# A two-layer mixer trunk in fp32 by split halves: the sample's output projection in seven half products, with the scale by token and the first results moved between engines

## The chip, the cores and the metric

The kernel runs on one core of one Trainium2 chip. The metric is the device time of one execution, in microseconds. The engines are TensorE (PE, with PEld for its weight loads), VectorE (DVE), ScalarE (ACT), GpSimd (POOL) and SyncE (SP), which issues most DMAs.

## The reference

A prompt of 512 tokens and a sample of 1024 tokens go through the same two layers, in fp32, width 1024:

```python
hn = rmsnorm(h, ln1[i])
z = hn @ w_in[i]
q, k, v, ga, uf, gf, mga, mgf = jnp.split(z, SPLIT_IDX, axis=-1)
...
a = band_attention(q, k, v, sink[i]) * jax.nn.silu(ga)
f = fourier_mix(uf, w_fmix[i]) * jax.nn.silu(gf)
merged = jax.nn.sigmoid(mga) * (a @ w_ao[i]) + jax.nn.sigmoid(mgf) * (f @ w_fo[i])
h = h + merged @ w_out[i]
gate = jax.nn.sigmoid(rmsnorm(h, ln_pg[i]) @ w_pg[i])
h = h + (p[i].astype(h.dtype) @ w_pe[i]) * gate
```

After the layers a last RMSNorm gives the outputs. The attention is banded (128 tokens to each side), the Fourier branch is a two-dimensional transform by channel groups.

## The kernel before, in words

Activations lie with features on the 128 partitions and tokens along the row: a tile is 128x512, eight of them (KD) make the 1024 features of a chunk of 512 tokens. Chunk 0 is the prompt, chunks 1 and 2 (PAIR) the sample. Each fp32 operand is split in two parts (`hi_lo`): ACT casts the high half (L93), DVE or POOL subtracts it to give the low half (L94). A product of a 128x128 weight tile and a token tile is then three matmuls, high by high, high by low, low by high (L105, L106, L107 in `mm3_steps`).

A layer runs the prompt and then the sample. Stages of the sample: the input projection (L236), attention and Fourier mixing woven into it, then `merge` (L553 on). The input projection already uses seven half products in place of eight: class `Pair` takes two output tiles by two chunks as a 2x2 block product, with weight sums S1 to S4 and token sums T1 to T4, and adds the products' banks on DVE (L253, L257 and others).

`merge` first makes the branch products, for each output tile m and chunk c 12 matmuls for attention (`ao`) and 12 for Fourier (`fo`). DVE applies the gates (L568, L569) and adds the two (L576) into `merged`. Then the 16 merged tiles are split. The output projection follows: for each m and chunk 24 matmuls in one PSUM bank, 384 a layer, and DVE adds a quarter of the bank to the old h (L594), the residual. `Norm.add` squares each new tile on ACT (L325) and sums the squares on DVE or POOL (L327, L330). The new h is split for the gate (L311 ACT, L312 DVE), and the gate's product runs as another 384 matmuls for both chunks; `finish` (L605 to L614) scales it by token (L610), applies tanh and adds the per-layer input (L612, L614). The scale by token is a row of 1/rms spread over the partitions by transposes into a PSUM bank (`Norm.scale_ps`) and copied to SBUF by DVE (L368). In the last layer `result` scales h for the output: for m%3 == 2 ACT multiplies by the norm's weight and POOL by the scale (L628, L629), else one DVE instruction (L631).

Weights of all these stages come from one stream (class `Weights`): DMAs of 4x128 rows by SP, split a few tiles ahead, `w_out` of the sample by POOL. The Tile framework sets the order of instructions of each engine from a timeline of its own at build time; `keep_in_program_order` pins some. PSUM has banks mm (3), sc (2), o (1) and misc (2); `any_ps` takes mm, sc and o in turn. `tick()` and `run` interleave other work, such as the prompt's normalizing for the next layer (L373), as steps.

## Time and profile before

| | us |
|---|---|
| median of 3 runs | 2195.79 (2192.51, 2195.79, 2196.96) |
| the profiled execution | 2191.9, of which its span 2190.1 |
| PE busy in the span | 2165.7 in 10273 matmuls |
| DVE, ACT, POOL busy | 1482.8, 1092.0, 284.6 |

The profile is of one execution, which took 2191.9 us, 3.9 less than the median; 1.8 us of it lie outside the span. The mean clock granted to PE is 0.999 of full speed. By the times of L594 the sample's output projection runs from about 952 to 1037 in layer 0 and from about 2001 to 2085 in layer 1. Busy times count matmuls by their modelled ends; how close together they start is read from the timeline.

### The profile page before, as it was taken

The page shows a single profiled execution, that of the slowest core. Times are in us where ns is not written, and L with a number is a line of the kernel's source. Part 1 is how long each engine was busy: PE and PEld are TensorE (multiplying, and loading weights), DVE is VectorE, ACT ScalarE, POOL GpSimd, SP SyncE. Part 2 cuts the span into 40 slices and gives each one's busy share as a digit, 9 for nine tenths or more (in the row PEclk, how much of TensorE's full clock was granted, in tenths as well). Part 3 has the DMA queues.
Part 4 walks back from the last instruction along what each step waited for, and adds up shares of the span by engine and source line. Part 5 has one row for each costly group of instructions (what it writes and reads, how often), then busy time and mean ns, then how long its engine had stood idle before and what let it go on. Part 6 is the DMA issues. An engine that isn't in the chain of part 4 may idle for free. (4 is left out here: it accounts for less than half of the span.)

```text
span 2190.1 us, 30146 instructions
## 1 busy us (share of the span) xinstructions
PE 2165.7 (99%) x10273; PEld 1806.4 (82%) x10273; DVE 1482.8 (68%) x2836; ACT 1092.0 (50%) x2338; POOL 284.6 (13%) x212
## 2 busy tenths in 40 slices
PE   9999999999999999999999999999999999999998
PEld 7878787888888888888888888888888888888887
DVE  5866686676678883464556676867766787855385
ACT  6576433566665464134324864336666644612252
POOL 0201100000002112221400010000000011241232
PEclk9999999999999999999999999999999999999999
DMA  8746454544448576531446455543444574753152
GB/s 313 265 136 205 171 192 145 166 140 137 159 142 290 198 251 213 199 105 64 151 159 202 152 193 172 185 153 130 161 146 151 192 283 137 267 197 116 44 169 100
DMA packets 242187, 380.71 MB, mean 174 GB/s; under 512 B 21233, under 2 KB 97649, under 8 KB 242033
## 3 DMA queue, kind: packets, MB, share of 16 engines
q1 hardware_dynamic: 234704, 365.80, 49.7%
q10 hardware_dynamic: 7328, 12.98, 1.6%
q8 instruction: 81, 1.33, 0.2%
q14 instruction: 74, 0.60, 0.1%
HBM read 270.17 MB, written 108.53 MB: 173 GB/s over the span
## 5 line engine op out<-in xcount | busy, mean ns | idle before, releaser
L236 PE MATMUL mm<-act,act 128*128 128x512 f32 x2856 | 692.6, 392 | 2.5 <-DVE scr L253 1.8
L236 PEld LDWEIGHTS mm<-act,act 128*128 128x128 f32 x2856 | 530.8, 188 | 111.2 <-ACT act L93 2.7
L105 PE MATMUL mm<-act,act 128*128 128x512 f32 x1384 | 542.9, 392 | 3.7 <-ACT scr L485 2.8
L107 PE MATMUL mm<-act,act 128*128 128x512 f32 x1384 | 541.2, 391 | 1.8 <-DVE act L94 1.8
L106 PE MATMUL mm<-act,act 128*128 128x512 f32 x1384 | 541.1, 391 | 0.0
L93 ACT CAST act<-act 128x512 fp32r<-128x512 f32 x574 | 329.1, 619 | 182.0 <-DMA act<-in_w_af 69.6
L94 DVE TENSOR_TENSOR act<-act,act 128x512 fp32r<-128x512 f32 x474 | 321.6, 713 | 33.8 <-ACT act L93 32.0
L107 PEld LDWEIGHTS mm<-act,act 128*128 128x128 f32 x1384 | 260.3, 188 | 56.9 <-DVE act L94 4.4
L105 PEld LDWEIGHTS mm<-act,act 128*128 128x128 f32 x1384 | 260.6, 188 | 56.4 <-ACT scr L485 4.2
L106 PEld LDWEIGHTS mm<-act,act 128*128 128x128 f32 x1384 | 260.5, 188 | 50.8
L93 ACT CAST act<-scr 128x512 fp32r<-128x512 f32 (+1 forms) x260 | 152.8, 615 | 127.7 <-DVE scr L435 58.0
L94 DVE TENSOR_TENSOR act<-scr,act 128x512 fp32r<-128x512 f32 x256 | 174.9, 704 | 51.6 <-ACT act L93 50.1
L94 POOL TENSOR_TENSOR act<-act,act 128x512 fp32r<-128x512 f32 x100 | 140.5, 1430 | 311.6 <-ACT act L93 249.3
L923 POOL TENSOR_TENSOR scr<-scr,scr 128x512 f32<-128x512 f32 x24 | 34.4, 1435 | 1036.6 <-DVE scr L920 1012.9
L325 ACT ACTIVATE scr<-act 128x512 f32<-128x512 f32 x103 | 63.8, 632 | 211.2 <-DVE act L594 142.6
L94 DVE TENSOR_TENSOR act<-misc,act 128x512 fp32r<-128x512 f32 x132 | 88.1, 685 | 72.0 <-ACT act L93 71.6
L93 ACT CAST act<-misc 128x512 fp32r<-128x512 f32 x132 | 73.9, 587 | 121.4 <-PE misc L909 119.2
L885 ACT ACTIVATE act<-act,stat 128x385 f32<-128x385 f32 (+1 forms) x192 | 110.6, 579 | 29.7 <-DVE stat L882 29.1
L882 DVE CUSTOM_DVE_ANT_0 act<-sc,mask_sb,nsink_sb 128x384 f32<-128x384 f32 (+1 forms) x192 | 104.2, 568 | 29.8 <-PE sc L874 29.2
L105 PE MATMUL sc<-act,act 128*128 128x512 f32 (+1 forms) x316 | 118.9, 376 | 0.0
L106 PE MATMUL sc<-act,act 128*128 128x512 f32 (+1 forms) x316 | 118.0, 374 | 0.0
L107 PE MATMUL sc<-act,act 128*128 128x512 f32 (+1 forms) x316 | 118.0, 373 | 0.0
(228 smaller groups left out, 2627.1 us busy)
## 6 DMA issues: line engine op xcount, KB each, us to landing
act<-in_w_in SPq DMA_DIRECT2D x136, 256.0 KB, 4.3
act<-in_w_in SPq DMA_DIRECT2D x68, 512.0 KB, 4.5
gt<-scr SPq DMA_DIRECT2D x96, 256.0 KB, 2.7
scr<-gt SPq DMA_DIRECT2D x96, 256.0 KB, 5.0
act<-in_w_pg SPq DMA_DIRECT2D x80, 256.0 KB, 3.4
act<-in_w_af SPq DMA_DIRECT2D x64, 256.0 KB, 5.3
act<-in_w_out SPq DMA_DIRECT2D x64, 256.0 KB, 5.1
pl<-scr ACTq DMA_DIRECT2D x48, 256.0 KB, 3.0
```

The source lines that it names most:

```text
L93: S.copy(hi, src)
L94: lo_eng.tensor_tensor(lo, src, f(hi), op=ALU.subtract)
L105: keep(PE.matmul(out, wh, xh, start=i == 0, stop=False))
L106: PE.matmul(out, wh, xl, start=False, stop=False)
L107: PE.matmul(out, wl, xh, start=False, stop=i == n - 1)
L236: PE.matmul(bank, w, v, start=first and k == 0 and n == 0, stop=k == 3 and n == 2, skip_group_check=True)
L325: S.activation(sq, h, AF.Square)
L882: V.tensor_tensor_reduce(out=pr[:, :W], in0=sc[:, :W], in1=msk, scale=-0.125, scalar=nsink_sb[:, l, head : head + 1], op0=ALU.add, op1=ALU ...
L885: S.activation(pr, pr, AF.Exp, bias=nmx[:, e], scale=-1.0, accum_out=rs[:, e])
L923: G.tensor_tensor(a2, a2, gate, op=ALU.mult)
```

## The change

For the sample, `merge` makes all attention halves first (L664 writes the gated product), then all Fourier halves (L666, L667). As the merged tiles of two chunks arrive, `made(m)` builds the token sums (L627 T1, L634 T2, L639 T3, L642 T4; rows 0 to 3 are tiles m and m+4) and splits them (L95 ACT, L96 DVE). The output projection is four calls of `Pair.alone`, each two output tiles by two chunks in seven half products of 12 matmuls (L237), 336 in a layer; DVE adds the banks (L291, L298, L299, L303, L307), then does the residual (L681). The weight sums and splits (`Pair.prepare`, L217 to L225, L96) are DVE's. The gate's weights come from a second stream whose first two steps fall in the last pair (`GATE_AT`), split by POOL. The scale for the gates is copied by ACT (L410); the first chunks' results read it from its bank, all on DVE (L731). In the input projection the sum c+v is made one product sooner. In the order of PE the 128x512 matmuls go from 8462 to 8366; in DVE's, 181 rows more.

```diff
@@ -222,22 +227,27 @@
...
+        def product(self, p, x, lead, pinned=False):
             def product(i, bank, xs, first):
                 if i == 2:
                     self.load(p + 1)
                 self.prepare(7 * p + i + lead)
                 for k, ((wh, wl), (xh, xl)) in enumerate(zip(self.w[7 * p + i], x[xs])):
                     for n, (w, v) in enumerate(((wh, xh), (wh, xl), (wl, xh))):
...
+            return product
+
...
@@ -252,14 +262,46 @@
...
+            V.tensor_tensor(v, c, v, op=ALU.add)
             yield from product(4, a, "B21", False)
             finish(0, 0, a, False)
-            V.tensor_tensor(v, c, v, op=ALU.add)
             finish(1, 1, v, True)
             yield
             yield from product(5, b, "T4", False)
             V.tensor_tensor(s1, b, s1, op=ALU.add)
             finish(1, 0, s1, True)
...
+        def alone(self, p, x, finish, lead):
+
+            a, b, c, d = (any_ps() for _ in range(4))
+            product = self.product(p, x, lead, True)
+            yield from product(0, a, "B11", True)
+            s1 = scr()
+            S.copy(s1, a)
+            yield
+            yield from product(1, c, "T1", True)
+            yield
+            yield from product(2, b, "T2", True)
+            q = scr()
+            V.tensor_tensor(q, b, s1, op=ALU.add)
+            yield
+            yield from product(3, a, "B21", False)
+            finish(0, 0, a, False)
+            yield
+            yield from product(4, b, "T3", False)
+            v = scr()
+            V.tensor_tensor(v, b, s1, op=ALU.add)
+            V.tensor_tensor(s1, c, v, op=ALU.add)
+            finish(1, 1, s1, True)
+            yield
+            yield from product(5, d, "T4", True)
+            V.tensor_tensor(v, d, v, op=ALU.add)
+            finish(1, 0, v, True)
...
@@ -567,35 +609,96 @@
...
+            pairs, t1 = Pair(outs_w, ("A11", "S1", "S2", "A12", "S3", "A22", "S4")), {}
+            late_rows = []
+            sums = {n: [] for n in ("B11", "T2", "T1", "T3", "B21", "T4", "B22")}
+
+            def made(m):
+                (b11, b12), (b21, b22) = (
+                    [merged[c][k // 2][:, k % 2, :] for c in chunks] for k in (m % 4, m % 4 + 4 if m > 3 else m % 4))
+                if m < 4:
+                    sums["B11"].append(two(halves(b11, V)))
+                    t1[m] = b11
+                    V.tensor_tensor(t1[m], b12, b11, op=ALU.subtract)
+                    sums["T1"].append(two(halves(t1[m], V)))
+                    return
+                late_rows.append((t1[m - 4], b12, b21, b22))
+                if m == 4 or m == 6:
+                    return
+                for t2, _, _, b22 in late_rows:
+                    V.tensor_tensor(t2, b22, t2, op=ALU.subtract)
+                    sums["T2"].append(two(halves(t2, V)))
+                for _, _, b21, _ in late_rows:
+                    sums["B21"].append(two(halves(b21, V)))
+                for _, b12, _, b22 in late_rows:
+                    V.tensor_tensor(b12, b22, b12, op=ALU.subtract)
+                    sums["T3"].append(two(halves(b12, V)))
+                for t2, _, b21, _ in late_rows:
+                    V.tensor_tensor(b21, b21, t2, op=ALU.subtract)
+                    sums["T4"].append(two(halves(b21, V)))
+                for _, _, _, b22 in late_rows:
+                    sums["B22"].append(two(halves(b22, V)))
+                late_rows.clear()
+
+            for i in range(2):
+                for m in range(KD):
                     if m % 2 == 0:
...
+                    n = KD * i + m - AHEAD
+                    if n == 0:
+                        pairs.load(0)
+                    if n > 1:
+                        pairs.prepare(min(n - 2, 4))
+                    for c in chunks:
+                        if i == 0 and m % 2 == 0:
+                            merged[c].append(big([P, 2, T]))
+                        g, s, out = scr(), merged[c][m // 2][:, m % 2, :], bank()
+                        SY.dma_start(g, GT[c][2 * m + i])
+                        mm3(out, w[m % 2 * 4 :][:4], parts[c][4 * i :][:4])
+                        if i == 0:
+                            V.scalar_tensor_tensor(s, g, 1.0, out, op0=ALU.add, op1=ALU.mult)
+                        else:
+                            V.scalar_tensor_tensor(g, g, 1.0, out, op0=ALU.add, op1=ALU.mult)
+                            V.tensor_tensor(s, s, g, op=ALU.add)
+                        tick()
+                        yield
+                    if i:
+                        made(m)
         hs, norm, rb = {c: [] for c in chunks}, {c: Norm() for c in chunks}, {}
...
+
+        def residual(m, c, out, in_sbuf=False):
+            old = scr()
+            SY.dma_start(old, x[c, m] if l == 0 else H[c][m])
+            if m // 2 == len(hs[c]):
+                hs[c].append(big([P, 2, T]))
+            h = hs[c][m // 2][:, m % 2, :]
+
+            V.scalar_tensor_tensor(h, out, 0.25, old, op0=ALU.mult, op1=ALU.add)
+            norm[c].add(h)
+
...
+        else:
+            following = gate_ws.start()
+            for p in range(KD // 2):
+                for n, _ in enumerate(pairs.alone(p, sums, lambda i, j, out, sb: residual(2 * p + i, chunks[j], out, sb), 3)):
+                    if p == KD // 2 - 1 and n in GATE_AT:
+                        next(following, None)
+                    tick()
+                    yield
+            ws = gate_ws
...
@@ -361,11 +403,11 @@
-        def scale(self):
+        def scale(self, copy=V.tensor_copy):
             rb_ps = pst("misc")
             self.scale_ps(rb_ps)
             rb = scr()
-            V.tensor_copy(rb, rb_ps)
+            copy(rb, rb_ps)
             return rb
@@ -604,7 +707,7 @@
-                rb[c] = norm2[c].scale()
+                rb[c] = norm2[c].scale(S.copy)
@@ -618,17 +721,14 @@
...
 
-            r = norm[c].scale()
+            r = pst("misc")
+            norm[c].scale_ps(r)
             for m in range(KD):
                 after(1 + m // 2, lambda m=m: result_tile(c, m, r))
 
         def result_tile(c, m, r):
             o, h, g = scr(), hs[c][m // 2][:, m % 2, :], ln_sb[:, 4, m : m + 1]
-            if m % 3 == 2:
-                S.activation(h, h, AF.Copy, scale=g)
-                G.tensor_tensor(o, h, r, op=ALU.mult)
-            else:
-                V.scalar_tensor_tensor(o, h, g, r, op0=ALU.mult, op1=ALU.mult)
+            V.scalar_tensor_tensor(o, h, g, r, op0=ALU.mult, op1=ALU.mult)
             SY.dma_start(y[c, m], o)
 
         keep = tc.keep_in_program_order
```

Two places of the order of instructions, both in layer 0. First, DVE where the branch products end and the output projection begins. `act_` and `scr_` are SBUF tiles, `mm_`, `sc_`, `o_` PSUM banks. Before, from the last gated products (L569) through the last sum and splits to the first residuals (L594):

```order
L569 SCALAR_TENSOR_TENSOR scr_9094<-scr_9094,mm_9098 128x512
L94 TENSOR_TENSOR act_9153<-act_8593,act_9153 128x512
L94 TENSOR_TENSOR act_9156<-act_8745,act_9156 128x512
L576 TENSOR_TENSOR act_9049<-scr_9093,scr_9094 128x512
L94 TENSOR_TENSOR act_9159<-act_8745,act_9159 128x512
L94 TENSOR_TENSOR act_9162<-act_8897,act_9162 128x512
L94 TENSOR_TENSOR act_9165<-act_8897,act_9165 128x512
L94 TENSOR_TENSOR act_9168<-act_9049,act_9168 128x512
L94 TENSOR_TENSOR act_9171<-act_9049,act_9171 128x512
L594 SCALAR_TENSOR_TENSOR act_9210<-sc_9183,scr_9184 128x512
```

Every split stands ahead of the first residual, and nothing else comes between. In the change, from the last T4 sum to the sum c+v of the first pair (L299); `act_9264` is the low half of A22 of the first pair, `o_9232` its bank c:

```order
L642 TENSOR_TENSOR act_8759<-act_8759,act_8602 128x512
L96 TENSOR_TENSOR act_9213<-act_8619,act_9213 128x512
L96 TENSOR_TENSOR act_9217<-act_8759,act_9217 128x512
L681 SCALAR_TENSOR_TENSOR act_9299<-sc_9230,scr_9297 128x512
L96 TENSOR_TENSOR act_9221<-act_8759,act_9221 128x512
L96 TENSOR_TENSOR act_9224<-act_8776,act_9224 128x512
L96 TENSOR_TENSOR act_9227<-act_8776,act_9227 128x512
L96 TENSOR_TENSOR act_9264<-act_8678,act_9264 128x512
L298 TENSOR_TENSOR scr_9318<-mm_9231,scr_9246 128x512
L96 TENSOR_TENSOR act_9282<-scr_8794,act_9282 128x512
L96 TENSOR_TENSOR act_9303<-act_9260,act_9303 128x512
L299 TENSOR_TENSOR scr_9246<-o_9232,scr_9318 128x512
```

The splits of late token sums now run on beside the first products, with the banks' sums (L298, L299), a residual (L681) and weight splits (`act_9264`, `act_9282`, `act_9303`) between and behind them.

Second, DVE in the middle of the output projection. Before, residuals, splits of the prompt's tiles for the next layer (L94) and sums of squares (L330):

```order
L594 SCALAR_TENSOR_TENSOR act_9410<-mm_9383,scr_9384 128x512
L94 TENSOR_TENSOR act_9416<-act_7286,act_9416 128x512
L94 TENSOR_TENSOR act_9460<-act_7444,act_9460 128x512
L330 TENSOR_TENSOR scr_9258<-scr_9258,scr_9412 128x512
L94 TENSOR_TENSOR act_9519<-act_7444,act_9519 128x512
L594 SCALAR_TENSOR_TENSOR act_9378<-sc_9428,scr_9429 128x512
L330 TENSOR_TENSOR scr_9212<-scr_9212,scr_9456 128x512
L594 SCALAR_TENSOR_TENSOR act_9410<-mm_9463,scr_9464 128x512
```

Here only L594 belongs to the product itself. In the change, the first half of the third pair:

```order
L291 TENSOR_TENSOR scr_9587<-mm_9531,scr_9549 128x512
L681 SCALAR_TENSOR_TENSOR act_9607<-o_9530,scr_9605 128x512
L96 TENSOR_TENSOR act_9612<-act_9568,act_9612 128x512
L372 TENSOR_TENSOR scr_9301<-scr_9301,scr_9609 128x512
L298 TENSOR_TENSOR scr_9627<-mm_9531,scr_9549 128x512
L299 TENSOR_TENSOR scr_9549<-sc_9532,scr_9627 128x512
L681 SCALAR_TENSOR_TENSOR act_9632<-scr_9549,scr_9630 128x512
L303 TENSOR_TENSOR scr_9627<-mm_9533,scr_9627 128x512
L217 TENSOR_TENSOR scr_9637<-act_9569 128x512
L372 TENSOR_TENSOR scr_9325<-scr_9325,scr_9634 128x512
L681 SCALAR_TENSOR_TENSOR act_9607<-scr_9627,scr_9656 128x512
L96 TENSOR_TENSOR act_9640<-scr_9637,act_9640 128x512
```

The residual reads a bank or a sum from SBUF, the prompt's tiles are gone from here, and weight sums (L217) and splits (L96) have come in.

## Rows read from the trace of the kernel before

**Rows 1.** The page, parts 1 and 2: busy time; PE and clock in slices
```profile
PE 2165.7 (99%) x10273; PEld 1806.4 (82%) x10273; DVE 1482.8 (68%) x2836; ACT 1092.0 (50%) x2338; POOL 284.6 (13%) x212
...
PE   9999999999999999999999999999999999999998
...
PEclk9999999999999999999999999999999999999999
```

**Rows 2.** PE's waits: line, awaited, total us, times, longest us
```profile
PE o L914 <- ACT act L93: 4.1, 4, 1.5
PE mm L105 <- ACT scr L485: 2.8, 4, 1.1
PE mm L107 <- DVE act L94: 1.8, 4, 0.6
PE mm L236 <- DVE scr L253: 1.8, 2, 0.9
```

**Rows 3.** Windows in both output projections: us, busy by engine, PEclk, DMA share, GB/s
```profile
960.00:1040.00 80.00, 80.00 (x355) 66.27 (x354) 40.81 (x62) 31.23 (x54) 18.66 (x15) 1.00 0.19 64
2000.00:2080.00 80.00, 80.00 (x354) 66.25 (x353) 27.27 (x39) 21.93 (x38) 21.11 (x16) 1.00 0.23 75
```

**Rows 4.** Groups by line: PE, layer 0, branch products to gate
```profile
L105 PE MATMUL mm<-act,act 128*128 128x512 f32 x273 | 106.6, 391 | 0.0
```

**Rows 5.** Timeline of PE: start, duration; first and last of eight matmuls
```profile
1749.72 0.39 PE L106 MATMUL mm<-act,act 128*128 128x512 f32 x1
...
1751.31 0.39 PE L107 MATMUL mm<-act,act 128*128 128x512 f32 x1
```

**Rows 6.** Timeline of DVE: start, duration, line; instructions that wait for nothing
```profile
1334.74 1.88 DVE L94 TENSOR_TENSOR act<-act,act 128x512 fp32r<-128x512 f32 x3
...
1744.78 3.20 DVE L94 TENSOR_TENSOR act<-act,act 128x512 fp32r<-128x512 f32 x5
1747.89 0.68 DVE L253 TENSOR_TENSOR scr<-mm,scr 128x512 f32<-128x512 f32 x1
```

**Rows 7.** The page, part 5: count, busy us, mean ns, idle before
```profile
L93 ACT CAST act<-act 128x512 fp32r<-128x512 f32 x574 | 329.1, 619 | 182.0 <-DMA act<-in_w_af 69.6
L94 DVE TENSOR_TENSOR act<-act,act 128x512 fp32r<-128x512 f32 x474 | 321.6, 713 | 33.8 <-ACT act L93 32.0
...
L94 POOL TENSOR_TENSOR act<-act,act 128x512 fp32r<-128x512 f32 x100 | 140.5, 1430 | 311.6 <-ACT act L93 249.3
```

**Rows 8.** Groups by line: layer 0's output projection, the scale's copy
```profile
L368 DVE COPY scr<-misc 128x512 f32<-128x512 f32 x1 | 0.7, 678 | 0.0
```

**Rows 9.** Single lines: durations in ns, least/median/longest
```profile
L631 DVE SCALAR_TENSOR_TENSOR scr<-act,ln_sb,scr x12: 742/744/1884, 1930.8 to 2171.7; 128x512 f32<-128x512 f32 x12
...
L629 POOL TENSOR_TENSOR scr<-act,scr x4: 1289/1292/1738, 1930.9 to 2159.3; 128x512 f32<-128x512 f32 x4
...
L612 DVE SCALAR_TENSOR_TENSOR scr<-scr,scr x46: 673/692/1775, 807.3 to 2166.5; 128x512 f32<-128x512 f32 x46
```

**Rows 10.** Window in layer 0's gate, columns as rows 3
```profile
1040.00:1126.00 86.00, 86.00 (x393) 71.41 (x392) 48.30 (x77) 27.19 (x46) 23.08 (x18) 1.00 0.44 150
```

**Rows 11.** Windows at a fall of the clock, columns as rows 3
```profile
201.00:202.00 1.00, 0.64 (x2) 0.54 (x3) 1.00 (x3) 1.00 (x4) 1.00 (x2) 0.50 1.01 377
...
204.00:206.00 2.00, 2.00 (x9) 1.61 (x8) 1.76 (x7) 1.61 (x4) 0.00 (x0) 0.92 0.85 211
```

**Rows 12.** Timeline of PE there; in brackets idle time and releaser
```profile
201.36 0.79 PE L105 MATMUL mm<-act,act 128*128 128x512 f32 x1 [1.06 <-ACT scr L485]
...
202.38 0.63 PE L107 MATMUL mm<-act,act 128*128 128x512 f32 x1
202.81 0.63 PE L105 MATMUL mm<-act,act 128*128 128x512 f32 x1
```

**Rows 13.** Window with POOL busy, layer 1's prompt, columns as rows 3
```profile
1900.00:1910.00 10.00, 10.00 (x46) 8.29 (x45) 9.62 (x8) 4.73 (x10) 9.66 (x6) 1.00 0.64 199
```

**Rows 14.** Groups by line: DVE, layer 0, branch products to gate
```profile
L94 DVE TENSOR_TENSOR act<-act,act 128x512 fp32r<-128x512 f32 x38 | 29.8, 817 | 2.5 <-issue 1.3 <-ACT act L93 1.0
```

More of the change, by code (lines that the diff above doesn't have):

```diff
@@ L29 @@
 LAST = 2
+AHEAD = 4
+GATE_AT = (4, 8)
 NF = 2
@@ L235, in product, with steps @@
                     for n, (w, v) in enumerate(((wh, xh), (wh, xl), (wl, xh))):
-                        PE.matmul(bank, w, v, start=first and k == 0 and n == 0, stop=k == 3 and n == 2,
-                                  skip_group_check=True)
+                        ins = PE.matmul(bank, w, v, start=first and k == 0 and n == 0, stop=k == 3 and n == 2,
+                                        skip_group_check=True)
+                        if pinned and k == n == 0:
+                            tc.keep_in_program_order(ins)
                     if k == 1:
                         yield
+            return product
+        def steps(self, p, x, finish, lead):
+            a, b, c = pst("mm"), pst("mm"), pst("mm")
+            product = self.product(p, x, lead)
             yield from product(0, a, "B11", True)
@@ L262, in steps @@
             finish(1, 0, s1, True)
+            yield
+            yield from product(6, c, "B22", False)
+            V.tensor_tensor(q, c, q, op=ALU.add)
+            finish(0, 1, q, True)
+            yield
[24 more added lines that the diff above has]
+            finish(1, 0, v, True)
             yield
@@ L551, in mixed, with merge @@
             yield
-    def merge(l, chunks, parts, ws, bank, groups):
+    def merge(l, chunks, parts, ws, bank, groups, outs_w=None, gate_ws=None):
         last = l == DEPTH - 1
@@ L556, in merge @@
         outs, gates = {c: [] for c in chunks}, {c: [] for c in chunks}
-        for m in range(KD):
-            w = ws.get()
-            for c in chunks:
+        if len(chunks) == 1:
+            for m in range(KD):
+                w, (c,) = ws.get(), chunks
                 ga, gf = scr(), scr()
@@ L581, in merge @@
-        hs, norm, rb = {c: [] for c in chunks}, {c: Norm() for c in chunks}, {}
-        for m in range(KD):
-            w = ws.get()
-            for c in chunks:
+                V.tensor_tensor(gf, ga, gf, op=ALU.add)
+                outs[c].append(two(halves(gf, V)))
+                yield
+        else:
[29 more added lines that the diff above has]
+            for i in range(2):
+                for m in range(KD):
+                    if m % 2 == 0:
+                        w = ws.get()
+                    n = KD * i + m - AHEAD
[15 more added lines that the diff above has]
+                        tick()
+                        yield
+                    if i:
+                        made(m)
@@ new lines, in merge @@
+        hs, norm, rb = {c: [] for c in chunks}, {c: Norm() for c in chunks}, {}
+        def residual(m, c, out, in_sbuf=False):
[6 more added lines that the diff above has]
+            norm[c].add(h)
+        if len(chunks) == 1:
+            for m in range(KD):
+                w, (c,) = ws.get(), chunks
@@ L598, in merge @@
-                yield
+                residual(m, c, out)
+                gates[c].append(split(hs[c][m // 2][:, m % 2, :], 2 + l, m))
+                yield
+        else:
+            following = gate_ws.start()
[4 more added lines that the diff above has]
+                    tick()
+                    yield
+            ws = gate_ws
@@ L1157, in streams, with whole, w_outs @@
         last = l == DEPTH - 1
-        tail = [w_af[l, m] for m in range(KD)] + [w_out[l, m] for m in range(KD)]
-        gate = [w_pg[l, m] for m in range(KD)]
-        return tail + gate + tail + (gate + gate if last else gate)
+        af = [whole(w_af[l, m]) for m in range(KD)]
+        af2 = [[w_af[l, m + i][:, r] for i in range(2)] for r in (slice(0, 4), slice(4, 8)) for m in range(0, KD, 2)]
+        out = [whole(w_out[l, m]) for m in range(KD)]
+        gate = [whole(w_pg[l, m]) for m in range(KD)]
+        return af + out + gate + af2, (gate + gate if last else gate + [whole(w) for w in w_ins(l + 1)])
+    def whole(w):
+        return w[:, 0:4], w[:, 4:8]
+    def w_outs(l):
+        return [w_out[l, m] for m in range(KD)]
     def w_ins(l):
@@ L1165, in trunk @@
     parts, tiles, rbs = [], [], []
-    ws = Weights(w_ins(0), ((V, V),) * 3)
+    ws = Weights([whole(w) for w in w_ins(0)], ((NMT, (V, V)),))
     def opening():
@@ L1224, in trunk @@
         if not last:
-            aux = [(prompt_normed(parts, l + 1, norm[0], hs[0]), 2 * 2 * KD, 0.4)]
+            aux = [(prompt_normed(parts, l + 1, norm[0], hs[0]), 2 * 2 * KD + 14 * 4 + 6, 0.5)]
             run(pe, [])
-        run(merge(l, PAIR, fx, ws, any_ps, ((1,), (2,)) if last else (PAIR,)), aux)
+        run(merge(l, PAIR, fx, ws, any_ps, ((1,), (2,)) if last else (PAIR,), w_outs(l), ws2), aux)
+        ws = ws2
         hs, norm = done.pop()
```

50 lines of the change are left out of this document (17 added, 33 removed).

## The prediction

> **What bounds the kernel now.** I read the page first: TensorE (PE) is busy in 99% of the span, in every one of the 40 slices, and PEclk, the clock granted to it, reads 9 in tenths throughout; VectorE (DVE) is busy in 68%, ACT in 50%, POOL in 13% [rows 1]. So the time is the number of matmuls by their pitch, and the little that PE waits. PE's waits come second: the longest four entries make 10.5 us in all, and none stands in the output projection [rows 2]. Third, the two output projections themselves: in 80 us of each PE is busy for 80.00 at clock 1.00, DVE for 40.81 in layer 0 and 27.27 in layer 1, and in the whole stretch from branch products to gate of layer 0 the largest matmul group has 0.0 idle ahead of it [rows 3, 4]. Fourth, the pitch: matmuls of 128x512 start at 1749.72, 1749.95, ... 1751.31, seven steps in 1.59 us, 0.227 us each (the 391 ns of a row are its duration, which overlaps the next) [rows 5]. A matmul removed there is worth 0.227 us, as long as nothing else becomes late.
>
> **What the change removes.** A sample layer's output projection has 16 output tiles of 8x3 matmuls, 384. Now it has 4 pairs of 7 half products of 4x3, 336. That is 48 less in each of two layers: 96 x 0.227 = **21.8 us**, all of it on PE's path. The branch products keep their 384 matmuls, only in another order (all attention halves, then all Fourier halves).
>
> **What it adds, on DVE.** Per layer: 16 sums of token tiles (L627, L634, L639, L642), 12 more splits of them (28 for 16), 16 sums of weights (L217 to L225), 28 weight splits that were 16 of POOL's, 20 additions of products (L291 to L307): 92 instructions, 184 in all. A pair of the new stage gives DVE 24: 7 weight splits, 4 weight sums, 5 product sums, 4 residuals, 4 sums of squares. Price: DVE instructions of this shape last 0.69 to 0.71 us, but where none waits the next starts sooner: three begun at 1334.74 end 1.88 later, five begun at 1744.78 end 3.20 later and the row behind them starts 3.11 after the first, so about 0.60 us of DVE each, ends 0.60 and 0.69 [rows 6, 7]. I take 0.602 in a burst and 0.62 in the pairs: 24 x 0.62 = 14.9 us, against 84 x 0.227 = 19.05 us of PE. Pairs 2 to 4 are covered with 4 us to spare, at 0.69 (16.6) too.
>
> **Where it is not covered: the start of the output projection.** The token sums of rows 2 and 3 (of 4 pairs of token tiles) need the last Fourier tiles. Let 0 be the end of the last branch matmul. Tiles end every 12 x 0.227 = 2.72 us; DVE keeps in step up to the second chunk's tile 5, four tiles from the end, at 4 x 2.72 = 10.9 before 0. From that row (L666 on scr_9073) to the low half of A22, the split on act_9264, DVE has 42 instructions in the order of the change (its second fence on the burst shows the end of them): 42 x 0.602 = 25.3, and some 0.2 for pairs that depend on each other, so ready at +14.6. PE wants it in the third matmul of product 5: 5 x 12 x 0.227 + 0.45 = 14.05. **0.6 us of stall.** The last T2 half is the 29th: 29 x 0.602 - 10.9 = 6.6, wanted in product 2 at 7.7, no stall. Product 6 writes the bank that L299 must first have read; four rows behind the 42, that ends at 17.05, and PE comes at 16.9: 0.15. So about 0.8 us per layer, **1.6 us** in two. The lower bound is 0 (PE's other stages of these layers begin without a wait [rows 4]); the upper is the pitch of 0.69, priced below.
>
> **The other parts.** *ACT*: 24 casts more per layer of 0.62 us [rows 7] and the copies L285; in a pair 7 casts, 4 squares, one copy, 12 x 0.62 = 7.4 of 19.05: covered. *Scale by token* (L410) is copied by ACT: 0.68 us [rows 8] moves from one engine with idle time to another, and its readers stand behind a first gate product of 24 matmuls, 5.4 us; nothing. *Results of chunks 0 and 1*: four STT more on DVE, 0.74 to 1.88 us each, for four products of POOL at 1.29 [rows 9]; they feed stores under the last chunk's matmuls and hold one misc bank longer; between 0 and +1, I take 0. *SP*: 16 loads of 128x1024 in place of 32 of 128x512, the first of them issued under the attention halves; the 16 DMA engines are a fifth busy here (share 0.19, 0.23 [rows 3]); nothing. *POOL* loses 32 weight splits of 1.43 us [rows 7] and has nothing left to do in the output stage until the gate's weights, split from product 4 of the last pair. *The prompt's normalizing for layer 1*, which stood in this stage of layer 0, comes under the gate, where DVE was busy 48.30 of 86 us [rows 10]; some 24 rows at 0.7 make 65 of 86; nothing. *In the input projection* the sum c+v comes one product sooner; PE waited 1.8 us on L253 in all [rows 2]: between 0 and -1.8, I take 0, since that row itself stays.
>
> **Sum.** -21.8 + 1.6 = -20.2 us. The profiled execution took 2191.9, so 2171.7; the median of the three runs, 2195.79, stands 3.9 above it, and the forecast is made against that: **2175.6 us**.
>
> **Rivals.** *A: DVE instructions don't overlap in the burst.* At 0.69 the 29th row is ready at 9.1 plus 0.3 for the dependent pairs, 1.7 late; the 42nd another 2.7 late by then, L299 0.6: 5.0 per layer, 10.0 in all, gain 11.8, **2184.0**. [...] The trace speaks against it where nothing is waited for [rows 6]; for it speaks that many rows of the burst wait for ACT's casts.
> *B: the clock falls behind the stalls.* [...]
> *C: everything is hidden*, since DVE is further ahead than I reckon: 21.8, **2174.0**.
> *D, slower: DVE sets the pace of the whole stage.* Beside POOL, DVE's rows stretch: in 1900 to 1910 POOL is busy 9.66 and DVE's 8 rows take 9.62 us, 1.20 each, and L612 has a median of 0.69 but a longest of 1.78 [rows 9, 13]. A pair costs PE 24 x m - 19.05 when the mean m of a DVE row passes 0.79; the gain of 2.7 per pair is used up at 0.907. At 1.0 it is 8 x 4.95 - 21.8 = +17.8: **2213.6**. [...] Against D: the change takes POOL's work out of just this stage; and even now, with POOL busy for 18.66 of 80 us beside it [rows 3], DVE's splits around this stage average 0.82 [rows 14], which would cost 8 x 0.63 = 5.0 of the 21.8.
> That the change doesn't do what it says can be left out: the order of PE has 96 matmuls less.
>
> **How the numbers follow.** Forecast 0.46, A 0.19, B 0.13, C 0.12, D 0.05; 0.05 for a part of the gain lost in a way I don't see (a bank, a load), 2187 to 2195. What a measurement can tell from no change is 0.2%, 4.4 us, so faster means under 2191.4. All of the first four are: 0.90; the unseen counts as the same, 0.05, D as slower, 0.05. The range goes from C less the 3.3 us by which one run of before lay under the median (2170.7, so 2171) to A and its spread, 2186; D and the unseen stay outside.
>
> **Signs.** Right: 96 matmuls less on PE; no wait of PE in pairs 2 to 4; in pair 1 of each layer a wait on a DVE split (L96) of under 1 us at product 5, and one on L299 of about 0.2; DVE busy some 0.75 to 0.8 of the stage; PEclk 1.00. Several us on L96 at products 2 and 5 make it A; a clock under 1 behind them B; no wait C; waits in every pair, DVE rows over 0.8 and DVE full, D. The forecast is wrong if the new stage isn't 10 us shorter in each layer, or if the gate or the tail behind it gives that back.

## The result, and the profile after

| | before | after |
|---|---|---|
| median, us | 2194.15 (4 runs, 2191.66 to 2196.96) | 2176.1 (4 runs, 2175.44 to 2179.12) |
| ratio | | 0.9921 (0.9909 to 0.9934) |
| profiled execution, its span | 2191.9, 2190.1 | 2175.55, 2173.5 |

One run more of the kernel before came in beside the runs of the changed one. The medians lie 18.0 us apart; the ratio is 17.3 us, with an interval of 14.5 to 20.0; the two spans are 16.6 apart. The forecast was 20.2 faster, at 2175.6. That the time itself came within 0.5 us is partly luck: the median of before came out 1.6 lower with the fourth run, and the gain was 2 to 3 us short.

The page of the changed kernel, parts 1 and 2 (busy time by engine; PE and its granted clock in 40 slices):

```profile
PE 2144.5 (99%) x10177; PEld 1787.0 (82%) x10177; DVE 1588.9 (73%) x3017; ACT 1124.7 (52%) x2395; POOL 245.2 (11%) x176
...
PE   9999999999999999999999999999999999999998
...
PEclk9999999999999999999999999999999999999999
```

Against [rows 1], PE has 96 matmuls less and is busy 21.2 us less, DVE 106 us more, POOL 39 less; PE is still busy in every slice. The longest waits of PE, with those of [rows 2] that have stayed:

```profile
PE o L1014 <- ACT act L95: 4.1, 4, 1.5
PE mm L107 <- ACT scr L527: 2.8, 4, 1.1
PE mm L107 <- ACT scr L367: 2.3, 1, 2.3
PE mm L237 <- DVE act L96: 2.0, 2, 1.0
PE mm L109 <- DVE act L96: 2.0, 4, 0.6
PE mm L237 <- DVE scr L263: 1.8, 2, 0.9
```

Two entries are new: 2.3 us once on ACT's L367, and twice 1.0 on DVE's L96. The second was forecast, the first was not.

The timeline of PE in the output projection of layer 0 (start, duration, line, x: matmuls in the row; in brackets the idle time before and its releaser), and DVE beside it:

```profile
950.70 2.88 PE L237 MATMUL sc<-act,act 128*128 128x512 f32 x12
...
961.58 3.33 PE L237 MATMUL mm<-act,act 128*128 128x512 f32 x14
965.91 2.56 PE L237 MATMUL mm<-act,act 128*128 128x512 f32 x10 [1.00 <-DVE act L96]
968.41 3.00 PE L237 MATMUL o<-act,act 128*128 128x512 f32 x12
...
1028.37 0.61 PE L107 MATMUL sc<-act,act 128*128 128x512 f32 x2
...
963.37 2.48 DVE L96 TENSOR_TENSOR act<-act,act 128x512 fp32r<-128x512 f32 x4
965.78 0.68 DVE L298 TENSOR_TENSOR scr<-mm,scr 128x512 f32<-128x512 f32 x1
```

The stage starts at 950.70 and the gate's first matmul comes at 1028.37: 77.67 us, where before 384 matmuls at the 0.227 of [rows 5] took 87.04, by PE's timeline from 949.04 to 1036.08. So 9.4 of the 10.9 us are there. 1.5 are lost in the first pair: 84 matmuls should end at 950.70 + 19.05 = 969.75, the second pair starts at 971.25 (the 1.00 in brackets, 0.23 in the ten matmuls behind it, which take 2.50, and small delays up to the second pair). The split that PE waits for is the last of the four L96 in the row at 963.37, which ends at 965.85, 15.2 after the stage's start where the prediction had 14.6. In layer 1 the stage is as long. Pairs 2 to 4 have no wait; pairs 2 and 3, by windows (us, busy and instructions of PE, PEld, DVE, ACT, POOL, clock, DMA share, GB/s):

```profile
971.00:1009.00 38.00, 38.00 (x169) 31.48 (x168) 29.86 (x48) 13.86 (x24) 0.00 (x0) 1.00 0.24 77
```

48 DVE instructions for two pairs, 29.86 of 38 us. Twice 9.4 is 18.8; the spans differ by 16.6. The largest loss elsewhere is 2.3 us in the prompt's gate of layer 0, some 137 us ahead of the stage that the change is about:

```profile
811.14 0.39 PE L109 MATMUL mm<-act,act 128*128 128x512 f32 x1
813.84 0.47 PE L107 MATMUL mm<-act,act 128*128 128x512 f32 x1 [2.31 <-ACT scr L367]
...
799.44 0.62 ACT L95 CAST act<-act 128x512 fp32r<-128x512 f32 x1
803.83 0.59 ACT L410 COPY scr<-misc 128x512 f32<-128x512 f32 x1 [3.77 <-PE misc L404]
...
800.78 0.69 DVE L96 TENSOR_TENSOR act<-act,act 128x512 fp32r<-128x512 f32 x1
804.45 1.29 DVE L713 TENSOR_TENSOR scr<-scr,scr 128x512 f32<-128x512 f32 x2 [2.99 <-ACT scr L410]
...
813.01 0.68 DVE L713 TENSOR_TENSOR scr<-mm,scr 128x512 f32<-128x512 f32 x1
```

The same place in the kernel before:

```profile
802.48 0.68 DVE L94 TENSOR_TENSOR act<-scr,act 128x512 fp32r<-128x512 f32 x1
804.09 0.69 DVE L368 COPY scr<-misc 128x512 f32<-128x512 f32 x1 [0.92 <-PE misc L362]
...
809.94 0.68 DVE L610 TENSOR_TENSOR scr<-mm,scr 128x512 f32<-128x512 f32 x1
```

ACT's copy of the scale (L410) waits 3.77 us for PE's transposes, with casts of the next tiles queued behind it; DVE then idles 2.99, all of the gate's DVE work comes late, and at 811 PE waits 2.31 us. Before, splits of the next tiles were done ahead of the copy (the last at 802.48), and the instruction that empties the first matmul bank (L610, now L713, the one with `mm` on the right) started at 809.94 in place of 813.01. For the wait at 811 the profile names L367, a square that neither reads nor writes a bank; L713 empties a bank of the kind that PE's next product writes and ends at 813.69, 0.07 ahead of L367. So the wait is put down to L713 here, by the program and not by the profile.

By the spans 2.2 us are missing. The other stretches differ as well, by up to about 1 us each way (the stage starts 1.7 later than before and not 2.3), and these small differences nearly cancel; they were not followed up.

### The profile page after: what moved, and what is told of

It is laid out like the page before. It is cut to its first block, busy times and chain, and to the rows that moved or that the text cites. A ratio compares the mean times of both kernels' runs of the same rounds, so it can differ in the third digit from the quotient of the medians.

```text
span 2173.5 us, 30130 instructions
## 1 busy us (share of the span) xinstructions
PE 2144.5 (99%) x10177; PEld 1787.0 (82%) x10177; DVE 1588.9 (73%) x3017; ACT 1124.7 (52%) x2395; POOL 245.2 (11%) x176
## 4 chain that ended last, share of the span: by engine, by line
PE 77%; DVE 5%; ACT 1%; DMA 1%; issue 1%; SPq 0%; DVEq 0%; ACTq 0%
PE mm L237 29%; PE mm L107 9%; PE mm L108 9%; PE mm L109 9%; PE o L1014 2%; PE sc L974 2%; PE sc L237 2%; PE misc L1009 2%; PE sc L107 2%; PE sc L109 2%; PE sc L108 2%; DVE act L96 2%; PE o L237 1%; PE o L109 1%; PE o L108 1%; PE o L107 1%
## 5 line engine op out<-in xcount | busy, mean ns | idle before, releaser
L237 PE MATMUL mm<-act,act 128*128 128x512 f32 x3144 | 761.2, 392 | 4.5 <-DVE act L96 2.0
L237 PEld LDWEIGHTS mm<-act,act 128*128 128x128 f32 x3144 | 584.7, 188 | 125.4 <-ACT act L95 2.9
L107 PE MATMUL mm<-act,act 128*128 128x512 f32 x1256 | 492.4, 393 | 6.0 <-ACT scr L527 2.8
L109 PE MATMUL mm<-act,act 128*128 128x512 f32 x1256 | 491.2, 391 | 2.0 <-DVE act L96 2.0
L108 PE MATMUL mm<-act,act 128*128 128x512 f32 x1256 | 491.6, 391 | 0.0
L95 ACT CAST act<-act 128x512 fp32r<-128x512 f32 x590 | 339.8, 621 | 172.0 <-DMA act<-in_w_af 47.1
L96 DVE TENSOR_TENSOR act<-act,act 128x512 fp32r<-128x512 f32 x522 | 353.9, 710 | 32.3 <-ACT act L95 31.2
L107 PEld LDWEIGHTS mm<-act,act 128*128 128x128 f32 x1256 | 236.5, 188 | 54.1 <-ACT scr L527 4.2
L109 PEld LDWEIGHTS mm<-act,act 128*128 128x128 f32 x1256 | 236.3, 188 | 51.9 <-DVE act L96 4.5
L108 PEld LDWEIGHTS mm<-act,act 128*128 128x128 f32 x1256 | 236.5, 188 | 45.9
L95 ACT CAST act<-scr 128x512 fp32r<-128x512 f32 (+1 forms) x292 | 172.8, 617 | 147.2 <-DVE scr L477 57.2
L96 DVE TENSOR_TENSOR act<-scr,act 128x512 fp32r<-128x512 f32 x288 | 200.2, 715 | 50.8 <-ACT act L95 48.7
L367 ACT ACTIVATE scr<-act 128x512 f32<-128x512 f32 x103 | 63.8, 632 | 170.6 <-DVE act L681 94.6
L96 POOL TENSOR_TENSOR act<-act,act 128x512 fp32r<-128x512 f32 x68 | 104.8, 1570 | 350.0 <-ACT act L95 326.5
L96 DVE TENSOR_TENSOR act<-misc,act 128x512 fp32r<-128x512 f32 x132 | 88.3, 687 | 71.9 <-ACT act L95 71.5
L95 ACT CAST act<-misc 128x512 fp32r<-128x512 f32 x132 | 73.9, 587 | 121.2 <-PE misc L1009 119.0
L990 ACT ACTIVATE act<-act,stat 128x384 f32<-128x384 f32 (+1 forms) x192 | 95.9, 573 | 12.8 <-DVE stat L988 12.8
L1014 PE MATMUL o<-act,act 128*128 128x512 f32 x256 | 92.3, 408 | 4.1 <-ACT act L95 4.1
L974 PE MATMUL sc<-act,scr 128*128 128x384 f32 (+1 forms) x384 | 85.6, 328 | 1.9 <-DVE stat L982 1.7
```

The costliest lines, as they stand in the source:

```text
L95: S.copy(hi, src)
L96: lo_eng.tensor_tensor(lo, src, f(hi), op=ALU.subtract)
L107: keep(PE.matmul(out, wh, xh, start=i == 0, stop=False))
L108: PE.matmul(out, wh, xl, start=False, stop=False)
L109: PE.matmul(out, wl, xh, start=False, stop=i == n - 1)
L237: ins = PE.matmul(bank, w, v, start=first and k == 0 and n == 0, stop=k == 3 and n == 2, skip_group_check=True)
```

## The experiments

Times are read against the kernel before in the same comparison, by ratios; runs of one kernel spread over some 2 to 4 us.

**Engine or place: three kernels.** The first puts the copy back on DVE in the changed kernel.

```diff
-                rb[c] = norm2[c].scale(S.copy)
+                rb[c] = norm2[c].scale()
```

> The changed kernel with one undo: the scale by token for the gates is copied by DVE again instead of ACT. Theory P (place): the 2.3 us wait of PE in the prompt's gate of layer 0 comes from where the copy stands, ahead of casts and splits that could run while the copy waits for PE's transposes; it stands just as early on DVE here, so the wait stays, 1.5 to 3 us near 811 us, and the time stays at 2176 within 1.5. Theory E (engine): the wait comes from ACT doing the copy; then it goes and the time falls by 2.3 to about 2173.8.

Measured: 2178.78 beside 2193.85, ratio 0.9932 (0.9919 to 0.9944); the changed kernel has 0.9921. The timeline of DVE and PE, and a window after the wait (columns as in rows 3):

```profile
799.63 1.28 DVE L96 TENSOR_TENSOR act<-scr,act 128x512 fp32r<-128x512 f32 x2
803.89 0.69 DVE L410 COPY scr<-misc 128x512 f32<-128x512 f32 x1 [2.97 <-PE misc L404]
...
814.48 0.47 PE L107 MATMUL mm<-act,act 128*128 128x512 f32 x1 [2.88 <-ACT scr L367]
...
816.00:819.00 3.00, 3.00 (x8) 2.32 (x8) 1.70 (x4) 1.79 (x4) 1.02 (x1) 0.50 0.31 111
```

DVE now waits 2.97 for the same transposes, and PE waits 2.88 in place of 2.31. In this execution the granted clock then reads 0.50 of full speed from 816 to 819. So the engine isn't the cause. The time rose by 2.4 us by the ratios, with intervals that overlap, where one theory had it unchanged within 1.5 and the other had it fall: beside the longer wait this build has one of 1.77 us on an ACT cast at 1326 in layer 1, which the changed kernel doesn't have.

The second leaves the copy on ACT, and restores something that I hadn't noted in the change: `residual` issues the load of the old h behind the product, for the prompt too; before, it stood ahead of the matmuls.

```diff
                 out = bank()
+                old = scr()
+                SY.dma_start(old, x[c, m] if l == 0 else H[c][m])
                 yield from mm3_steps(out, w, outs[c], 4)
                 tick()
-                residual(m, c, out)
+                residual(m, c, out, old=old)
```

> The changed kernel with one undo: in the prompt's output projection the load of the old h is issued ahead of the product's matmuls again, as before the change; ACT keeps the copy of the scale, but the order of instructions now has that copy seven casts later on ACT, behind the casts of the next tiles. Theory P (place): no wait of PE over 0.5 us between 805 and 815 us, the time falls by about 2.3 to 2173.8. Theory E (engine): ACT still copies, so the wait of 2.3 us stays and the time is 2176.

Measured: 2174.19 beside 2193.85, ratio 0.9910 (0.9897 to 0.9924). Its ACT and its largest matmul group around that place:

```profile
801.73 0.62 ACT L95 CAST act<-act 128x512 fp32r<-128x512 f32 x1
805.05 0.59 ACT L410 COPY scr<-misc 128x512 f32<-128x512 f32 x1 [2.70 <-PE misc L404]
...
L109 PE MATMUL mm<-act,act 128*128 128x512 f32 x70 | 27.4, 392 | 0.0
```

The copy still waits, 2.70 us, but the casts are done by then, and no matmul has idle time ahead of it from 780 to 830. By the profile the 2.3 us are gone. Its output stage of layer 0 starts at 947.91, 2.8 us ahead of the changed kernel's. The ratio says 2.4 with intervals that overlap, but in the profiled execution the lead is lost again: this build too has the wait of 1.77 us near 1322 in layer 1, the clock falls behind it (matmuls start 0.43 us apart from 1324.12 to 1326.68), and layer 1's stage starts at 1991.53 for 1990.80. Its order differs there too.

The third is the kernel before with the copy on ACT alone.

```diff
-                rb[c] = norm2[c].scale()
+                rb[c] = norm2[c].scale(S.copy)
```

> The kernel before with one part of the change alone: the scale by token for the gates is copied by ACT. Theory P: the copy stands late on ACT (behind the casts), so nothing is lost, 2194 within 1.5, the same waits of PE as before. Theory E: a new wait of some 2.3 us in the prompt's gate of layer 0, about 2196.5.

Measured: 2195.3 beside 2193.85, ratio 1.0007 (0.9998 to 1.0015), and PE has no wait in the prompt's gate. (It has two waits elsewhere that the kernel before doesn't have, 2.10 us at 16 and again 1.77 in layer 1, at 1333; the time alone doesn't tell the two theories apart here.) Place, not engine, three times out of three. A later kernel, the fastest one below with the copy on DVE but late in its order, says the same from the other side.

One rival these runs don't separate: in every kernel here the late load of the old h and the early copy come together, so the load itself could be what is late. The traces speak against it. The residual does wait longer for that load, 4.37 us in the changed kernel and 3.12 before, but the transposes are no later: the copy starts at 803.83, before at 804.09. What is late is the work queued behind the copy.

**What the wait in the first pair is for.** First A22, the split that PE waits for, was taken out of DVE's burst.

```diff
-                        pairs.prepare(min(n - 2, 4))
+                        pairs.prepare(min(n - 2, 5))
```

> The changed kernel with the sixth weight block of the first pair (A22) prepared under the Fourier halves, not in the output projection. Theory B (burst): the wait of 1.0 us at product 5 of the first pair stands in each sample layer because A22's low half is the last of DVE's burst of 42 rows; taken out of the burst, both waits go, 2.0 to 2.3 us, about 2173.8, and no new wait over 0.3 us stands in the first pair. Rival: the burst as a whole is late, the wait only moves to another token sum (T4 or T3) or to L299 and the time falls by less than 0.7.

Measured: 2176.21 beside 2193.85, ratio 0.9919 (0.9906 to 0.9933): no gain that can be told, though the stage is 0.6 us shorter in each layer. PE's timeline:

```profile
960.92 5.60 PE L237 MATMUL mm<-act,act 128*128 128x512 f32 x24
967.14 3.00 PE L237 MATMUL o<-act,act 128*128 128x512 f32 x12 [0.62 <-DVE scr L299]
```

The wait of 1.00 on A22 is gone and one of 0.62 on L299 stands at the next product. The rival was right: what is late is the whole queue, and its end is whichever row PE needs last. Then both weight blocks, A22 and S4, were prepared early (`min(n - 2, 6)`), on top of the kernel with the old h first.

> The kernel of e12_old_first with the sixth and the seventh weight block of the first pair (A22 and S4) both prepared under the Fourier halves. Theory B2 (a queue of 46 rows on DVE: the wait at product 5 or 6 is for whatever stands at its end): three weight rows less ahead of L299 than now are enough for both points, the waits of 1.0 us on L96 and of 0.6 us on L299 are gone from the first pair of both layers, and the time is 2.0 to 2.3 under e12_old_first, about 2171.9 where that stands at 2174.2. Rival: the wait moves on to a token sum (T4, B22) and less than 0.8 is won.

Measured: 2173.12 beside 2192.72, ratio 0.9907 (0.9893 to 0.9922). Both waits are gone from the first pair in both layers, and the stage is 0.95 us shorter in each, 1.9 in all; the ratio shows 0.7 of it, within its interval, so the time doesn't tell the two theories apart; the profile does, by the waits. Of the 1.5 us lost in the pair, some 0.55 stay as delays too short to be listed as waits. Its PE timeline, to be held against that of the changed kernel:

```profile
958.03 5.60 PE L237 MATMUL mm<-act,act 128*128 128x512 f32 x24
963.74 3.04 PE L237 MATMUL o<-act,act 128*128 128x512 f32 x12
```

**What a DVE instruction costs in a pair.** Fourteen useless additions more per pair, in pairs 2 to 4:

```diff
+            def extra():
+                for _ in range(2 if p else 0):
+                    V.tensor_tensor(junk, s1, s1, op=ALU.add)
...
             yield from product(1, c, "T1", True)
+            extra()
```

> The changed kernel with 14 useless additions more on DVE in each of pairs 2 to 4 (2 behind each half product, 84 in all; the outputs don't change). A pair has 38 rows then. At 0.60 us a row that is 22.9 us against PE's 19.05, so DVE sets the pace and the time rises by 6 x 3.8 = 23 less some slack at the ends, 16 to 23, to 2192 to 2199. At 0.69 us a row (rival A, no overlap of DVE's instructions) it is 26.2, +43, to 2219. If it stays under +5, DVE had more slack than its rows show.

Measured: 2215.83 beside 2192.72, ratio 1.0105 (1.0088 to 1.0121), 40 us over the changed kernel, near the figure for 0.69 us. But the profile says that the price was 0.60 all the same. DVE in pair 3, and windows in pairs 3 and 4:

```profile
994.55 0.68 DVE L96 TENSOR_TENSOR act<-scr,act 128x512 fp32r<-128x512 f32 x1
995.15 0.68 DVE L219 TENSOR_TENSOR scr<-scr,act 128x512 f32<-128x512 f32 x1
995.75 0.68 DVE L320 TENSOR_TENSOR scr<-sc,scr 128x512 f32<-128x512 f32 x1
996.35 0.68 DVE L290 TENSOR_TENSOR scr<-scr 128x512 f32<-128x512 f32 x1
...
995.00:1017.00 22.00, 19.17 (x79) 15.44 (x78) 21.65 (x36) 6.31 (x11) 0.00 (x0) 0.93 0.22 72
1018.00:1044.00 26.00, 19.50 (x80) 15.78 (x79) 25.65 (x36) 11.98 (x21) 6.63 (x4) 0.88 0.45 142
```

Durations are 0.68, starts 0.60 apart. DVE is full, 36 instructions in 22 us, and pair 3 takes 23.73 us, 38 at 0.62. Pair 4 takes 27.52: the gate's weights are then split by POOL (6.63 us), and 36 DVE instructions take 26 us, 0.72 each. With the backlog handed on and POOL beside, the two stages are 33 us longer in place of 16 to 23; the other 7 are elsewhere. PE waits once for 2.2 us on ACT's L513 and 2.1 more in all on ACT casts (L95) than in the changed kernel, and the mean clock of this execution is 0.993 for 0.999. The expectation priced three equal pairs and missed the last.

**POOL beside DVE.** The weight splits of pairs 2 to 4 were given to POOL.

```diff
-                hi_lo(t[:, 0], t[:, 1], a[name], V)
+                hi_lo(t[:, 0], t[:, 1], a[name], self.eng if b > 6 else V)
```

> The changed kernel with the weight splits of pairs 2 to 4 (21 in each layer) on POOL instead of DVE. Theory S (slack): DVE has 17 rows per pair left; even at 1.0 us each beside POOL that is 17 of 19 us, so PE waits nowhere in pairs 2 to 4 and the time stays within 1.5 of 2176. Rival D (contention): DVE's rows beside POOL take over 1.1 us on the mean, PE waits in each pair and the time rises by 5 or more.

Measured: 2178.19 beside 2192.72, ratio 0.9930 (0.9915 to 0.9945), between the two expectations. Pairs 2 and 3, and one of their groups (mean ns of one behind the comma):

```profile
972.00:1010.00 38.00, 38.00 (x169) 31.46 (x168) 28.27 (x35) 14.13 (x24) 21.20 (x14) 1.00 0.27 83
...
L222 DVE TENSOR_TENSOR scr<-act,act 128x512 f32<-128x512 f32 x2 | 3.6, 1780 | 0.0
L681 DVE SCALAR_TENSOR_TENSOR act<-scr,scr 128x512 f32<-128x512 f32 x6 | 4.1, 685 | 0.1
...
979.17 1.78 DVE L369 SCALAR_TENSOR_TENSOR scr<-scr,scr 128x512 f32<-128x512 f32 x1
981.49 0.69 DVE L291 TENSOR_TENSOR scr<-mm,scr 128x512 f32<-128x512 f32 x1 [0.55 <-PE mm L237]
```

35 instructions in 28.27 us, 0.81 each, where 48 took 29.86 without POOL: DVE gets 13 instructions less and almost no time back. POOL is busy for 21.20 of the 38 us. Held against POOL's own rows, the DVE instructions with two inputs in SBUF that lie wholly beside POOL's take 1.78 us, six of them (L222, L225 and a sum of squares in each pair); L291 and L307, which read one input from a bank, take 0.69 there too, and so do the L681, which POOL meets for part of their time or not at all. PE waits 0.2 us on L299 once more per layer, and the stage is 0.4 longer. So beside POOL those with two inputs in SBUF took 1.78 us for 0.69, and there was slack for it.

**What a matmul is worth.** The first half product of pairs 2 to 4 made twice:

```diff
             yield from product(0, a, "B11", True)
+            if p:
+                yield from product(0, a, "B11", True)
```

> The changed kernel with the first half product of pairs 2 to 4 made twice (72 matmuls more, the second overwrites the first; the outputs don't change). If PE bounds these pairs and each matmul is worth 0.227 us, the time rises by 16.3 to 2192.4, between 15 and 18. If something else sets the pace there, it rises by less than 12.

Measured: 2200.09 beside 2192.72, ratio 1.0033 (1.0020 to 1.0046), 25 us over the changed kernel. In the output stages the expectation holds: from first to last matmul they are 8.13 and 8.11 us longer, 36 matmuls at 0.226 each. As a whole it missed, 25 for 15 to 18; the other 8 are elsewhere. One of the places, where the changed kernel doesn't wait, is the input of layer 1:

```profile
1148.26 0.79 PE L107 MATMUL mm<-act,act 128*128 128x512 f32 x1 [1.75 <-ACT act L95]
```

Another wait like it, of 1.77 us, stands at 1338.54. Two waits of 3.5 us in all, and the granted clock, 0.69 from 814 to 818 and from 1146 to 1150 and 0.50 from 1150 to 1154 (some 4.5 us of these 12, where the changed kernel's profile has no fall), make up about the other 8 in this execution. The clock isn't the whole account: another execution of this kernel, with a mean clock of 0.999, has a span of 2198.7 for the 2198.3 of this one. That the framework ordered other stages anew behind an edit in one is shown by the waits; how much of the 8 it cost, not.

**The other small part.** The results of chunks 0 and 1 as before, two of eight tiles by ACT and POOL:

```diff
-            r = pst("misc")
-            norm[c].scale_ps(r)
+            r = norm[c].scale()
...
+            if m % 3 == 2:
+                S.activation(h, h, AF.Copy, scale=g)
+                G.tensor_tensor(o, h, r, op=ALU.mult)
+            else:
+                V.scalar_tensor_tensor(o, h, g, r, op0=ALU.mult, op1=ALU.mult)
```

> The changed kernel with one undo: the first chunks' results are made as before (two of eight tiles by ACT and POOL, the scale copied to SBUF). Theory N (off the path): within 1.5 of 2176, the end of the kernel as long after the last matmul as now. Rival: the part mattered at the end; then the time moves by 3 or more.

Measured: 2182.5 beside 2193.18, ratio 0.9951 (0.9939 to 0.9964). The part that I had at nothing is worth 6 to 7 us in this kernel. DVE, POOL and PE in layer 1's attention halves, without the part and (behind the last dots) with it, in the changed kernel:

```profile
1923.31 0.69 DVE L410 COPY scr<-misc 128x512 f32<-128x512 f32 x1 [5.38 <-PE misc L404]
1924.04 6.94 DVE L734 SCALAR_TENSOR_TENSOR scr<-act,ln_sb,scr 128x512 f32<-128x512 f32 x4
1930.90 0.68 DVE L664 SCALAR_TENSOR_TENSOR act<-scr,mm 128x512 f32<-128x512 f32 x1
...
1924.08 2.98 POOL L732 TENSOR_TENSOR scr<-act,scr 128x512 f32<-128x512 f32 x2 [11.01 <-DVE scr L410]
1927.03 3.40 POOL L96 TENSOR_TENSOR act<-act,act 128x512 fp32r<-128x512 f32 x2
...
1931.63 0.50 PE L107 MATMUL mm<-act,act 128*128 128x512 f32 x1 [2.88 <-DVE act L664]
...
1932.80:1935.80 3.00, 3.00 (x9) 2.35 (x8) 2.15 (x4) 0.00 (x0) 0.00 (x0) 0.50 0.99 318
...
1922.96 4.04 DVE L731 SCALAR_TENSOR_TENSOR scr<-act,ln_sb,misc 128x512 f32<-128x512 f32 x6 [5.38 <-PE misc L404]
1926.92 0.68 DVE L664 SCALAR_TENSOR_TENSOR act<-scr,sc 128x512 f32<-128x512 f32 x1
```

DVE sits at the scale for 5.38 us in both, for the same transposes. Then four results, with two inputs in SBUF and beside POOL's two results and two splits, take 6.94 us, 1.74 each, where six of the changed kernel, with the scale in PSUM and POOL at rest, take 4.04. L664, which frees the banks of the attention halves, comes at 1930.90 in place of 1926.92, and PE, out of banks, waits 2.88; the clock fell behind it in this execution (0.50 from 1932.8 to 1935.8), and another 1.5 us are lost in waits of the last chunk's end. That the new branch order makes this part matter was tried from the other side, the part alone in the kernel before:

> The kernel before with one part of the change alone: the first chunks' results all on DVE, with the scale read from its bank. Theory C (cover): undoing this part in the changed kernel cost 6.4 us because there the results stand ahead of DVE instructions that free the banks of the attention halves; in the kernel before PE waits for no bank at that place, so the part alone is worth nothing but the end of the kernel, within 1.5 of the kernel before. Rival: the part is worth 4 to 6 us by itself, whatever the order of the branch products.

Measured: 2191.74 beside 2193.6, ratio 0.9995 (0.9986 to 1.0004), 1.1 us by the ratio: little or nothing. The part is cover for the change, not a gain of its own. Last, the seven half products without any of the small parts (the old h first, the copy on DVE, results as before, c+v late):

> The seven half products alone: the kernel of e12_old_first with the scale copied by DVE, the results by ACT and POOL, and the sum c+v at its old place. Theory M (matmuls): 96 matmuls at 0.227 us less two waits of 1.5 us in the first pairs, 18.8 us under the kernel before, 17 to 20, so about 2174.5 beside a kernel before of 2193.3; the other parts are worth nothing together. Rival: the parts carry some of the gain, and this kernel is less than 15 under before.

Measured: 2181.14 beside 2193.18, ratio 0.9941 (0.9928 to 0.9955): 13 us, not 17 to 20; the rival was right. The same wait of 2.88 us on L664 stands in it, with a granted clock of 0.57 from 1930 to 1934 and 0.58 from 1934 to 1938.

**The best.** The kernel with the old h first and the weights early, the copy late on DVE:

> The kernel of e14_weights_early with the scale copied by DVE; the order of instructions has the copy late on DVE (behind the splits), as the kernel before had. Theory P (place): no wait over 0.5 us in the prompt's gate of layer 0, and within 1.5 of e14_weights_early (2173.1). Rival: a copy on DVE costs the gates something; 2 or more slower.

Measured: 2172.3 beside 2193.18, ratio 0.9903 (0.9890 to 0.9917), 21.3 us under the kernel before and about 4 under the changed one, by ratios whose intervals overlap a little. PE has no wait in the prompt's gate, with the copy on DVE, and none in the first pairs. The wait of 1.77 us on an ACT cast in layer 1 stands here too, at 1320.

## Why the prediction was right, and where it wasn't

*Bound and gain.* Right. 96 matmuls less, the stage shorter by 9.4 us in each layer, PE's clock 1.00 in it, no wait in pairs 2 to 4; the experiment with matmuls added shows 0.226 us for each.

*The price of DVE.* Right, at 0.602 us. Where nothing is waited for, the next instruction starts 0.08 us before the end of the one ahead (0.68 us long, starts 0.60 apart), in the burst, in the pairs, and in the kernel with additions. A falls: it has 0.69 for each, and the 42 instructions of the burst took 25.8 us, 0.61 each.

*The start of the output projection.* The mechanism and the row were right (A22's split, the 42nd), the size too small: 1.5 us in place of 0.8 in each layer. The split came 0.6 us later than reckoned (15.2 for 14.6): the 42 instructions run from 940.02 to 965.85, 25.8 us for 25.5, and begin 10.7 ahead of the stage for 10.9. And the wait cost more than its idle time of 1.00, as the ten matmuls behind it took 2.50 for 2.27. That L299 was next, the prediction had as 0.15; it showed with 0.62 as soon as A22 was out of the way.

*The clock (B).* It didn't fall behind these waits: 1.00 from 964 to 972. It did behind longer ones of 1.8 to 2.9 us in several executions of the experiments (0.50 behind the 2.88 of the first and behind the 2.88 with the results as before, 0.69 and 0.50 behind the 1.75 with the matmuls added); in the changed kernel's own profile it stayed at 1.00 behind the 2.31.

*DVE beside POOL (D).* No POOL in the stage, so no sign of it; with POOL put there DVE's mean instruction rose to 0.81. The 0.907 that would have used up the gain was reckoned for 24 instructions in a pair; for the 17 or 18 left there, 0.81 makes some 14 of 19.05 us. Of the 92 added instructions of a layer, 20, the sums of products, read a bank: beside POOL L291, one of them, took 0.69 us, and L222, with two inputs in SBUF, 1.78.

*The step that failed: the list of the other parts, with "nothing" for the scale by token.* I named its readers and not what is queued behind it on its own engine. The copy waits 3.77 us for PE's transposes, and it now stands before casts that were ahead of it: five of them start at 804.84, where in the kernel before five start at 798.51. That is the 2.3 us. The edit that moved it was the load of the old h, which the list doesn't have, as I had not read it as a change for the prompt. Undone, the wait goes; with the copy back on DVE and the load late, it stays (2.88).

*The results, "between 0 and +1".* Right as a difference to the kernel before, wrong as an account of the change: without this part the new order of the branch products would lose 6 to 7 us. The sum held because the two parts came together.

*The sum c+v, one product sooner*, was taken as 0: PE's wait on it is 1.8 us in both profiles.

So the gain was 21.8 less 3.0 in the first pairs less about 2.3 in the prompt's gate: 16.5, against 16.6 in the spans and 17.3 by the ratio. That these come so close is in part chance, with small differences of up to 1 us in the other stretches. The forecast left out the last term and half of the first loss.

## What to carry to other kernels

Where PE is full, count the matmuls and believe the count; then read the order of instructions of the *whole* program against the old one, since a framework that orders by a timeline of its own may move a waiting instruction ahead of ready ones far from the edit. Of every instruction that waits for another engine ask what stands behind it in its queue. And a part of a change that is worth nothing alone may be what pays for another part: undo it within the change, not only alone.

## What the runs showed that I had not expected

Behind one and the same wait of PE the granted clock fell in some executions and not in others. The wait of 2.3 us in the prompt's gate stands unchanged in six of the profiles: from 814 to 818 the clock reads 1.00 in four, the changed kernel's among them, 0.74 in that with the splits on POOL and 0.69 in that with the matmuls added. A wait of some 1.07 us near 202 stands in all fourteen: from 201 to 206 the clock reads 1.00 throughout in four, and falls in ten (in the changed kernel 0.73 from 201 to 204 and 0.55 from 204 to 206).

What a fall costs: from 816 to 819 in the first experiment, at 0.50, matmuls start 0.43 us apart in place of 0.227, so these 3 us lose some 1.4. Part of the spread of the runs is this. Of the eleven runs of the results' part alone in the kernel before, the three with a mean clock of 1.000 have spans of 2188.8, 2188.8 and 2189.4, the other eight 2189.0 to 2192.8. It isn't all, as the kernel with the matmuls added shows. What decides whether the clock falls was not settled here.
